# Norm sums as column-tiled matmuls with a high and a low part, and attention's norms moved from the score stage into the output stage ahead of it

## The chip, the cores and the metric

One Trainium2 chip, the same program on all 8 cores (two dies of four), each core with its own sequence of the prompt group and its own 16 samples. The metric is the device time of the slowest core in microseconds. Executions come in a fast and in a slow state (in the slow one the cores of one die, in some runs of both, show a lower granted clock: the lowest core of each slow run has a mean of 0.811 to 0.971); every comparison below uses fast runs only.

## The reference, cut to what matters

Two layers, three sub-blocks each, every sub-block behind an RMSNorm over 1024 channels:

```python
def rmsnorm(x, g):
    xf = x.astype(jnp.float32)
    y = xf * lax.rsqrt(jnp.mean(xf * xf, axis=-1, keepdims=True) + EPS)
    return (y * g.astype(jnp.float32)).astype(x.dtype)
# per layer:
#   x = x + mixer(rmsnorm(x))          layer 0 pooling, layer 1 gated short convolution
#   x = x + mem_attend(rmsnorm(x))     256 memory tokens, 4 heads
#   x = x + sq_relu_mlp(rmsnorm(x))
```

## The kernel before

x lies in SBUF with channels on partitions, as 8 chunks of 128 channels by 2064 tokens, and is worked off in 5 tiles of 416 tokens (the last 400, 16 of them samples). The sum of squares over channels is a sum over partitions, so TensorE makes it: a 128x128 matrix of ones times the squared chunks, eight matmuls accumulating in one PSUM bank. Every partition of the bank then holds the same sum, and ScalarE turns it into `exp(-0.5*ln(sum/D + eps))`.

```python
    def norm_a(ti, U, n=None, parts=1):            # squares, on ACT
        ...
            act(U(sl(a, a + w), sl(0, n)), X(sl(a, a + w), sl(c0, c0 + n)), AF.Square)

    def norm_b(ti, grow, U, RSTD, n=None):
        norm_r(ti, U, RSTD, n)
        norm_s(ti, grow, U, RSTD, n)

    def norm_r(ti, U, RSTD, n=None):               # sums on PE, then ln and exp on ACT
        n = n or TILES[ti][1]
        bk = nxt()
        for c in range(NCH):
            mm(PSv(bk, 0, n), ONESB(), U(c, sl(0, n)), c == 0, c == NCH - 1)
        act(PSv(bk, 0, n), PSv(bk, 0, n), AF.Ln, scale=1.0 / D, bias=EPS)
        act(RSTD(sl(0, n)), PSv(bk, 0, n), AF.Exp, scale=-0.5)

    def norm_s(ti, grow, U, RSTD, n=None, cs=range(NCH)):   # scaling, eight DVE instructions
        for c in cs:
            stt(U(c, sl(0, n)), X(c, sl(c0, c0 + n)), G(c, sl(grow, grow + 1)), RSTD(sl(0, n)), ALU.mult, ALU.mult)
```

There are 25 such norms on a core: 1 in the prelude (attention's norm of the first tile), 18 for attention and MLP of the two layers, 6 in the conv stage. `nxt()` hands out PSUM banks in rotation. Attention runs as score stages S(k) (eight blocks m) and output stages O(k-1) (eight column blocks ec), interleaved. Small pieces hang between blocks; one is `step`, which starts a sample's attention, with eight dot products on DVE:

```python
        for k in range(NT):
            def mid_s(m, k=k):                     # after block m of score stage S(k)
                ...
                if k == 0:
                    ...
                    if m == 1:
                        N2a(1)                     # squares
                    if m == 4:
                        N2b(1)                     # sums and scaling
                    return
                if m == 2:
                    N2b(k + 1) if k + 1 < NT else N3b(0)
                ...
                if m == 5:
                    step()
            S(k, mid_s)
            ...
            if k > 0:
                O(k - 1, lambda ec: (trickle() if ec % 2 == 0 else pre() if ec == 1 else step() if ec == 3 else None))
```

The sample attention already uses column tiling: four matmuls with 16 output columns each, into four groups of 32 PSUM partitions:

```python
        def SB(b):
            for x in range(2):
                for h in range(4):
                    mmx(V(PS[32 * h:32 * h + NS, OBK, 0:257], ...), PBZ[b % 2](x * 4 + h), VS[b % 2](x, h, sl(0, 257)), ...)
```

In the conv stage each channel block c is 24 matmuls; DVE has a chain of six to eight instructions per block, and its last product (`gate`) frees the block's last PSUM bank.

The softmax here doesn't subtract the row's maximum and nothing guards it: scores larger than these inputs give would overflow.

Of the kernel before, what the change touches and what calls it, by code (L numbers as in the profile page):

```python
# [8 lines left out]
BF16 = mybir.dt.bfloat16  # L9
# [122 lines left out]
def build_program():  # L132
# [99 lines left out]
    def sl(a, b):  # L232
        return slice(a, b)

    def PSv(bank, a, b, m=128):
        return V(PS[0:m, bank, a:b], [(PSB + bank * 2048, PSB + (bank + 1) * 2048)], excl=True)
# [11 lines left out]
    def nxt():  # L248
        b = bank_ctr[0] % bank_mod[0]
        bank_ctr[0] += 1  # L250
        return b
# [39 lines left out]
    def mm(out, lhsT, rhs, start, stop):  # L291
        P.add(PE, "c", lambda e, o=out.ap, l=lhsT.ap, r=rhs.ap: e.matmul(out=o, lhsT=l, rhs=r, start=start, stop=stop),  # L292
              [lhsT, rhs], [out])
# [19 lines left out]
    def act(out, in_, func, scale=1.0, bias=0.0):  # L313
        rd = [in_]
        sc = scale
        if isinstance(scale, V):
            rd.append(scale)
            sc = scale.ap
        P.add(ACT, "c", lambda e, o=out.ap, i=in_.ap: e.activation(out=o, in_=i, func=func, bias=bias, scale=sc), rd, [out])  # L319
# [87 lines left out]
    def trickle():  # L407
        if pieces:
            name, kc = pieces.pop(0)
            if kc == 0:  # L410
                claim(name)
            dma(POOL, W(name)(kc), DV(wsrc_sq(wsrc[name])[:, kc, :]), f"w{slot_of[name]}")
# [10 lines left out]
    def norm_a(ti, U, n=None, parts=1):  # L423
        c0 = TILES[ti][0]
        n = n or TILES[ti][1]
        w = NCH // parts
        for a in range(0, NCH, w):
            act(U(sl(a, a + w), sl(0, n)), X(sl(a, a + w), sl(c0, c0 + n)), AF.Square)

    def norm_b(ti, grow, U, RSTD, n=None):  # L430
        norm_r(ti, U, RSTD, n)
        norm_s(ti, grow, U, RSTD, n)

    def norm_r(ti, U, RSTD, n=None):
        n = n or TILES[ti][1]
        bk = nxt()
        for c in range(NCH):
            mm(PSv(bk, 0, n), ONESB(), U(c, sl(0, n)), c == 0, c == NCH - 1)
        act(PSv(bk, 0, n), PSv(bk, 0, n), AF.Ln, scale=1.0 / D, bias=EPS)
        act(RSTD(sl(0, n)), PSv(bk, 0, n), AF.Exp, scale=-0.5)  # L440

    def norm_s(ti, grow, U, RSTD, n=None, cs=range(NCH)):
# [19 lines left out]
    def prelude():  # L462
# [238 lines left out]
        for k in range(4):  # L701
            extra[13 + k].append(lambda k=k: kv("wk0", mk_d, k))
        extra[11].append(lambda: norm_a(0, BUF[0], parts=2))
        extra[12].append(lambda: norm_r(0, BUF[0], RSTDE))
        for i in range(4):
            extra[13 + i].append(lambda i=i: norm_s(0, R_ATTN, BUF[0], RSTDE, cs=(2 * i, 2 * i + 1)))
        stA(0)
# [104 lines left out]
    def conv_nA(ti):  # L812
        norm_a(ti, CUT[ti % 2], parts=2)

    def conv_nB(ti):
        norm_b(ti, R_MIX + 1, CUT[ti % 2], RSTDQ)

# [64 lines left out]
    def conv_phase():  # L882
        conv_begin()
        for ti in range(NT):
            def mid(c, ti=ti):
                if c == 0 and ti:
                    conv_out(ti - 1)
                if ti == 0 and c == 2:
                    conv_state()
                if ti == 1 and c == 1:  # L890
                    conv_state2()
                if c == 2:
                    if ti == NT - 1:
                        norm_a(SEQS[1][0], BUF[0], parts=2)
                    elif ti:
                        conv_nA(ti + 1)
                if c == (4 if ti else 1):
                    first_norm(1, RSTDQ) if ti == NT - 1 else conv_nB(ti + 1)

            conv_in(ti, mid)  # L900
        free("cin_b")
        load("wq1")
# [18 lines left out]
    def attn_phase(l, fill=()):  # L921
# [26 lines left out]

        def N2a(k):
            norm_a(seq[k], BT[k % 2])  # L950

        def N2b(k):
            norm_b(seq[k], R_ATTN + l, BT[k % 2], RSTD)
# [35 lines left out]
        def O(k, mid):  # L989
            c0, _, n, _ = TILES[seq[k]]  # L990
            pt = PT[k % 2]
            for ec in range(NCH):
                bk = nxt()
                for m in range(NCH):
                    mm(PSv(bk, 0, n), VWO(m, sl(ec * 128, (ec + 1) * 128)), pt(m, sl(0, n)), m == 0, m == NCH - 1)
                tt(X(ec, sl(c0, c0 + n)), PSv(bk, 0, n), X(ec, sl(c0, c0 + n)), ALU.add)
                mid(ec)
# [100 lines left out]
        def N3a(ti):  # L1098
            norm_a(ti, BT[1] if ti == 0 else U3[ti], TILES[ti][2])

        def N3b(ti):
            norm_b(ti, R_FFN + l, BT[1] if ti == 0 else U3[ti], RSTDM if ti > 1 else RSTD, TILES[ti][2])

# [20 lines left out]
        def stB(q, ti, j, mid=None, cols=None):  # L1124
            c0, n, npmt, ns = TILES[ti]
            n = npmt if q == 0 else n
            a0, a1 = cols or (0, n)
            Wd = W(f"dn{l}_{q}")
            h = H[j % 2]
            for ec in range(NCH):  # L1130
                bk = nxt()
                for fc in range(NCH):
                    mm(PSv(bk, 0, a1 - a0), Wd(fc, sl(ec * 128, (ec + 1) * 128)), h(fc, sl(a0, a1)), fc == 0, fc == NCH - 1)
                tt(X(ec, sl(c0 + a0, c0 + a1)), PSv(bk, 0, a1 - a0), X(ec, sl(c0 + a0, c0 + a1)), ALU.add)
                if mid is not None:
                    mid(ec)
# [11 lines left out]
        def step():  # L1148
            if todo:
                todo.pop(0)[1]()  # L1150

        def pre():
            if todo and todo[0][0] is not None:
                todo[0][0]()

        for k in range(NT):
            def mid_s(m, k=k):
                if m % 2 and k:
                    trickle()
                if l == 0 and (k == 1 or k == 0 and m > 3):  # L1160
                    late.pop(0)()
                if k == 0:
                    if l == 1 and m == 1:
                        conv_tail()
                    if m == 1:
                        N2a(1)
                    if m == 4:
                        N2b(1)
                    if l == 1 and m == 6:
                        conv_tail2()  # L1170
                    return
                if m == 2:
                    N2b(k + 1) if k + 1 < NT else N3b(0)
                if l == 0 and k == 1:
                    return
                if m == 3:
                    pre()
                if m == 5:
                    step()

            if k == 1:
                QSAMP()
                if l == 0:
                    free("wv0")
                    load_slowly("dn0_0")
            S(k, mid_s)
            if l == 0 and k == 1:
                free("wo0")
                load_slowly("up0_1")
                SDK(0)  # L1190
                SDV(0)
            if k + 2 < NT:
                N2a(k + 2)
            elif k + 2 == NT:
                N3a(0)
            if k > 0:
                O(k - 1, lambda ec: (trickle() if ec % 2 == 0 else pre() if ec == 1 else step() if ec == 3 else None))
        SDK(n_att)

        def mid_o(ec):  # L1200
            if ec == 0:
                N3a(1)
            if ec % 2 == 0:
                trickle()
            if ec == 1:
                pre()
            if ec == 3:
                step()
            if ec == 5:
                N3b(1)  # L1210

        O(NT - 1, mid_o)
# [38 lines left out]
        for j, (q, ti) in enumerate(items):  # L1251
            if q == 0 and ti + 2 < NT:
                N3a(ti + 2)
            if j + 1 < len(items):
                q1, t1 = items[j + 1]
                stA(q1, t1, j + 1, mid_m)
                if t1 == NT - 1 and q1:
                    free(f"up{l}_{q1}")
                    if q1 < 3:
                        load(f"dn{l}_{q1 + 1}")  # L1260
            if q == 0 and ti + 2 < NT:
                N3b(ti + 2)
            yield ("A", j)
            if l == 1 and j == len(items) - 1:
                stB(q, ti, j, mid_m, (TAIL, n_last))
                yield ("T", j)
                stB(q, ti, j, mid_m, (0, TAIL))
            else:
                stB(q, ti, j, mid_m)
            if ti == NT - 1 and q:  # L1270
                free(f"dn{l}_{q}")
                if q < 2:
                    load(f"up{l}_{q + 2}")
            yield (q, ti)
# [34 lines left out]
    for at in attn_phase(0, kv1_fill()):  # L1309
        if at == ("A", 16):  # L1310
            conv["cin_c"] = load_u("cin_c", 0)
        if at == ("A", 18):
            conv["cin_h"] = load_u("cin_h", 1)
            load("cout")
            conv_nA(1)
        if at == (3, 2):
            conv_nA(0)
        if at == ("A", 18):
            conv_nB(0)
    conv_phase()  # L1320
    done = [0]
# [146 lines left out]
```

## Time and profile before

| | before |
|---|---|
| time, median of fast runs | 1622.3 us (first four runs) |
| PE busy | 97% |
| norm: PE time held by the eight matmuls | 1.41 us at 416 columns (1.30 to 1.35 on narrower tiles), 25 times |
| PE waits of all kinds between 110 and 1500 us, slowest core | about 7 us |

PE bounds this kernel.

The timeline of before, PE only, around one group of column-tiled sample matmuls (start, duration, group, count).

```profile
299.71 4.56 PE L292 MATMUL PS<-MEM 128*128 128x416 bf16 x25
304.20 0.40 PE L296 MATMUL PS<-MEM 128*16 128x257 bf16 x8
304.53 13.37 PE L292 MATMUL PS<-MEM 16*128 16x512 bf16 x74
```

Eight matmuls of 257 columns hold PE for 0.33 us, from 304.20 to 304.53. One after another they would take about 8 x 0.11 us (an estimate from the 176 ns from start to start at 416 columns). In the records four start 3 to 4 ns apart and the next four 113 ns after these. So four really run side by side. The extra time on entering and leaving comes once per group: 270 ns from the start before to the first of them, where 176 is usual, and 206 ns from the last to the next start, where 257 columns would take about 110 by the same estimate.

### The profile page before, as it was taken

Reading aid. Unit: us, or ns where it says so; the run is one execution under the profiler, and the core shown is the slowest. Engines: PE = TensorE matmul, PEld = TensorE weight load, DVE = VectorE, ACT = ScalarE, POOL = GpSimd, SP = SyncE. Lnnn points to the kernel's source line nnn. Section 1 sums busy time; section 2 is a strip of 40 time slices with the busy share of each in tenths; the row PEclk is TensorE's granted clock in tenths of the full one; section 3 lists DMA queues with packets and bytes.
Section 4 is the critical chain, followed back from the end, with each engine's and each line's share of the span. In section 5 each row is a group of like instructions: output and inputs, shape, how many; then the busy total and the mean of one; then the engine's idle time right before and its main releaser. Section 6 shows DMA issues by size and latency. Waiting matters only on the chain.

```text
span 1620.1 us, 28511 instructions; the slowest of 8 cores (1616.6 to 1620.1 us)
## 1 busy us (share of the span) xinstructions
PE 1568.4 (97%) x10162; PEld 912.5 (56%) x10168; DVE 848.8 (52%) x1899; ACT 555.8 (34%) x1046; POOL 113.7 (7%) x245
## 2 busy tenths in 40 slices
PE   4899999999999999999999999999999999999997
PEld 3775555555556655555555555555555655555565
DVE  4666675655443444445666664767465444442325
ACT  4755435441121221222223224533643112213453
POOL 2002121110000000000000001121110000000000
PEclk9999999999999999999999999999999999999999
DMA  8979793665537706067000009694555663000112
GB/s 221 211 123 170 153 189 61 122 141 84 85 65 130 120 1 105 14 92 109 1 1 1 0 1 170 118 205 94 120 118 73 97 105 53 14 1 1 40 66 106
DMA packets 87189, 145.13 MB, mean 90 GB/s; under 512 B 4350, under 2 KB 41470, under 8 KB 87036
## 3 DMA queue, kind: packets, MB, share of 16 engines
q0 software_dynamic: 67568, 84.08, 36.0%
q1 hardware_dynamic: 19484, 59.24, 11.0%
q8 instruction: 84, 1.38, 0.3%
q14 instruction: 53, 0.43, 0.1%
HBM read 212.42 MB, written 14.36 MB: 140 GB/s over the span
## 4 chain that ended last, share of the span: by engine, by line
PE 91%; DVE 2%; ACT 2%; DMA 2%; issue 2%; POOL 0%; DVEq 0%; ACTq 0%; SPq 0%; POOLq 0%
PE PS L292 88%; PE PS L296 2%; DVE MEM L327 2%; ACT MEM L319 1%; DMA MEM<-gv 1%; PE PS L301 1%; DMA MEM<-x 1%; ACT MEM L308 1%; DVE MEM L331 0%; DVE MEM L345 0%; DVE MEM L339 0%; ACT MEM L343 0%; POOL MEM L354 0%; DVEq L1362 0%; ACTq L1362 0%
## 5 line engine op out<-in xcount | busy, mean ns | idle before, releaser
L292 PE MATMUL PS<-MEM 128*128 128x416 bf16 (+5 forms) x9082 | 1495.1, 325 | 11.6 <-ACT MEM L319 3.9
L292 PEld LDWEIGHTS PS<-MEM 128*128 128x128 bf16 x9088 | 844.0, 98 | 650.6 <-issue 42.1
L319 ACT ACTIVATE MEM<-PS 128x416 f32<-128x416 f32 (+5 forms) x469 | 238.6, 510 | 650.1 <-PE PS L292 639.4
L331 DVE TENSOR_TENSOR MEM<-PS,MEM 128x416 f32<-128x416 f32 (+6 forms) x533 | 297.7, 574 | 264.7 <-PE PS L292 256.4
L331 DVE TENSOR_TENSOR MEM<-MEM 128x416 bf16<-128x416 f32 (+3 forms) x282 | 159.8, 583 | 196.9 <-ACT MEM L319 188.4
L327 DVE SCALAR_TENSOR_TENSOR MEM<-MEM 128x416 bf16<-128x416 f32 (+7 forms) x322 | 176.9, 601 | 128.7 <-ACT MEM L319 109.0
L319 ACT ACTIVATE MEM<-MEM 128x416 bf16<-128x416 f32 (+9 forms) x299 | 184.9, 630 | 147.7 <-DVE MEM L331 112.6
L304 DVE SCALAR_TENSOR_TENSOR MEM<-MEM,PS 128x256 f32<-128x256 f32 x256 | 105.1, 420 | 72.6 <-PE PS L292 49.4
L343 ACT COPY MEM<-PS 128x512 f32<-128x512 f32 (+3 forms) x73 | 39.1, 535 | 134.8 <-PE PS L292 121.6
L296 PE MATMUL PS<-MEM 128*128 128x128 bf16 (+4 forms) x896 | 60.7, 248 | 16.7 <-DVE MEM L339 7.8
L296 PEld LDWEIGHTS PS<-MEM 128*128 128x128 bf16 (+2 forms) x896 | 49.0, 107 | 30.3 <-issue 29.5
L345 DVE CAST MEM<-PS 128x512 bf16<-128x512 f32 (+1 forms) x68 | 43.0, 654 | 12.1 <-PE PS L292 12.1
L354 POOL DMA_DIRECT2D MEM<-cv x64 | 47.6, 744 | 13.8 <-PE PS L292 13.5
L343 ACT CAST MEM<-PS 128x512 bf16<-128x512 f32 (+3 forms) x57 | 30.7, 548 | 48.7 <-PE PS L292 47.9
L319 ACT ACTIVATE PS<-PS 128x416 f32<-128x416 f32 (+3 forms) x67 | 33.1, 494 | 40.0 <-PE PS L292 39.6
L327 DVE SCALAR_TENSOR_TENSOR MEM<-PS,MEM 128x1024 f32<-128x1024 f32 (+1 forms) x17 | 21.8, 1283 | 44.3 <-ACT MEM L319 44.3
L301 PE MATMUL PS<-MEM 128*128 128x128 f32 (+5 forms) x184 | 24.7, 275 | 16.9 <-DMA MEM<-gv 7.1
L351 POOL MEMSET MEM<- 128x4 bf16 (+1 forms) x96 | 15.0, 159 | 357.8 <-PE PS L296 307.5
L301 PEld LDWEIGHTS PS<-MEM 128*128 128x128 f32 (+5 forms) x184 | 20.5, 143 | 20.0 <-issue 18.5
L354 POOL DMA_DIRECT2D MEM<-w_up x36 | 20.6, 582 | 131.9 <-PE PS L292 131.9
L339 DVE TENSOR_SCALAR MEM<-MEM 128x1024 bf16<-128x1024 f32 (+1 forms) x18 | 17.9, 997 | 22.7 <-ACT MEM L319 22.7
L354 POOL DMA_DIRECT2D MEM<-w_down x22 | 13.8, 635 | 207.2 <-PE PS L292 163.1
(28 smaller groups left out, 137.4 us busy)
## 6 DMA issues: line engine op xcount, KB each, us to landing
MEM<-ck SPq DMA_DIRECT2D x64, 512.0 KB, 6.2
MEM<-cv POOLq DMA_DIRECT2D x64, 256.0 KB, 6.1
MEM<-w_down POOLq DMA_DIRECT2D x6, 2048.0 KB, 17.9
MEM<-x SPq DMA_DIRECT2D x16, 512.0 KB, 12.5
MEM<-w_kv POOLq DMA_DIRECT2D x4, 2048.0 KB, 19.0
MEM<-w_o POOLq DMA_DIRECT2D x4, 2048.0 KB, 24.6
MEM<-w_up POOLq DMA_DIRECT2D x32, 256.0 KB, 13.2
MEM<-w_up POOLq DMA_DIRECT2D x4, 2048.0 KB, 17.9
```

Of the source, the lines that this page charges most:

```text
L292: P.add(PE, "c", lambda e, o=out.ap, l=lhsT.ap, r=rhs.ap: e.matmul(out=o, lhsT=l, rhs=r, start=start, stop=stop), [lhsT, rhs], [out])
L296: P.add(PE, "c", lambda e, o=out.ap, l=lhsT.ap, r=rhs.ap: e.matmul(out=o, lhsT=l, rhs=r, start=start, stop=stop, is_transpose=is_transpose ...
L301: P.add(PE, "c", lambda e, o=out.ap, i=in_.ap, d=ident.ap: e.transpose(out=o, in_=i, identity=d), [in_, ident], [out])
L304: P.add(DVE, "c", lambda e, o=out.ap, a=in0.ap, b=in1.ap, c=acc.ap: e.scalar_tensor_tensor(out=o, in0=a, scalar=1.0, in1=b, op0=ALU.mult, ...
L308: P.add(ACT, "c", lambda e, o=out.ap, i=in_.ap, a=acc.ap: e.activation(out=o, in_=i, func=AF.Square, accum_out=a), [in_], [out, acc])
L319: P.add(ACT, "c", lambda e, o=out.ap, i=in_.ap: e.activation(out=o, in_=i, func=func, bias=bias, scale=sc), rd, [out])
L327: P.add(eng, "c", lambda e, o=out.ap, a=in0.ap, b=in1.ap: e.scalar_tensor_tensor(out=o, in0=a, scalar=sc, in1=b, op0=op0, op1=op1), rd, [out])
L331: P.add(eng, "c", lambda e, o=out.ap, a=in0.ap, b=in1.ap: e.tensor_tensor(out=o, in0=a, in1=b, op=op), [in0, in1], [out])
L339: P.add(eng, "c", lambda e, o=out.ap, a=in0.ap: e.tensor_scalar(out=o, in0=a, scalar1=sc, scalar2=None, op0=op0), rd, [out])
L343: P.add(ACT, "c", lambda e, o=out.ap, i=in_.ap: e.copy(out=o, in_=i), [in_], [out])
L345: P.add(eng, "c", lambda e, o=out.ap, i=in_.ap: e.tensor_copy(out=o, in_=i), [in_], [out])
L354: return P.add(q, "d", lambda e, o=out.ap, i=in_.ap: e.dma_start(out=o, in_=i), [in_], [out], chan=chan, after=after)
```

## The change

The intent: summing over partitions needs only one useful output column, so eight matmuls of 128 columns make the same sum 128 times. Take 32 columns, run four chunks side by side in four column groups, in two passes. This leaves four partial sums on the four partition groups. Split them into a bf16 high part (ACT copy) and a bf16 low part (DVE subtraction), and add and broadcast them with two full ones-matmuls. The sums are split in time: `norm_p` first, `norm_r` with the scaling some blocks later. Attention's norms also move from score stage S(k+1) into output stage O(k-1).

```diff
+    def norm_p(ti, U, RSTD, n=None):
+        n = n or TILES[ti][1]
+        bk = nxt()
+        for i in range(2):
+            for h in range(4):
+                mmx(V(PS[32 * h:32 * h + 32, bk, 0:n], PSv(bk, 0, 1).ivs, True), ONESB(sl(0, 32)), U(4 * i + h, sl(0, n)), i == 0, i == 1)
+        hi, lo = [T(RSTD.off + i * n * 2, BF16, [n]) for i in range(2)]
+        cp(hi(), PSv(bk, 0, n), eng=ACT)
+        tt(lo(), PSv(bk, 0, n), hi(), ALU.subtract)
+
     def norm_r(ti, U, RSTD, n=None):
         n = n or TILES[ti][1]
         bk = nxt()
-        for c in range(NCH):
-            mm(PSv(bk, 0, n), ONESB(), U(c, sl(0, n)), c == 0, c == NCH - 1)
-        act(PSv(bk, 0, n), PSv(bk, 0, n), AF.Ln, scale=1.0 / D, bias=EPS)
+        for i in range(2):
+            mm(PSv(bk, 0, n), ONESB(), T(RSTD.off + i * n * 2, BF16, [n])(), i == 0, i == 1)
+        act(PSv(bk, 0, n), PSv(bk, 0, n), AF.Ln, scale=1.0 / (32 * D), bias=EPS)
...  prelude
-        extra[12].append(lambda: norm_r(0, BUF[0], RSTDE))
+        extra[12].append(lambda: norm_p(0, BUF[0], RSTDE))
+        extra[13].append(lambda: norm_r(0, BUF[0], RSTDE))
...  conv stage
-                if c == (4 if ti else 1):
+                if c == (3 if ti else 0):
+                    if ti == NT - 1:
+                        norm_p(SEQS[1][0], BUF[0], RSTDQ)
+                    else:
+                        conv_nP(ti + 1)
+                if c == (5 if ti else 2):
                     first_norm(1, RSTDQ) if ti == NT - 1 else conv_nB(ti + 1)
...  score stage
-                    if m == 4:
+                    if m == 3:
+                        N2p(1)
+                    if m == 5:
                         N2b(1)
...
-                if m == 2:
-                    N2b(k + 1) if k + 1 < NT else N3b(0)
+                if k == 1 and m == 0:
+                    N2p(2)
+                if k == 1 and m == 2:
+                    N2b(2)
...  output stage
-                O(k - 1, lambda ec: (trickle() if ec % 2 == 0 else pre() if ec == 1 else step() if ec == 3 else None))
+                def mid_k(ec, k=k):
+                    ...
+                    if ec == 3:
+                        step()
+                    if k < NT - 1:
+                        if ec == 4:
+                            N2p(k + 2) if k + 2 < NT else N3p(0)
+                        if ec == 6:
+                            N2b(k + 2) if k + 2 < NT else N3b(0)
+
+                O(k - 1, mid_k)
...  MLP part: N3p before an output stage, N3b after its second block (cut)
```

More of the change, by code (lines that the diff above doesn't have):

```diff
@@ L813, in conv_nA, with conv_nP @@
         norm_a(ti, CUT[ti % 2], parts=2)
+    def conv_nP(ti):
+        norm_p(ti, CUT[ti % 2], RSTDQ)
     def conv_nB(ti):
@@ L950, in N2a, with N2p @@
             norm_a(seq[k], BT[k % 2])
+        def N2p(k):
+            norm_p(seq[k], BT[k % 2], RSTD)
         def N2b(k):
@@ L1099, in N3a, with N3p @@
             norm_a(ti, BT[1] if ti == 0 else U3[ti], TILES[ti][2])
+        def N3p(ti):
+            norm_p(ti, BT[1] if ti == 0 else U3[ti], RSTDM if ti > 1 else RSTD, TILES[ti][2])
         def N3b(ti):
@@ L1196, in attn_phase @@
             if k > 0:
-                O(k - 1, lambda ec: (trickle() if ec % 2 == 0 else pre() if ec == 1 else step() if ec == 3 else None))
+                def mid_k(ec, k=k):
+                    if ec % 2 == 0:
+                        trickle()
+                    if ec == 1:
+                        pre()
+                    if ec == 3:
[6 more added lines that the diff above has]
+                O(k - 1, mid_k)
         SDK(n_att)
@@ L1208, in mid_o @@
                 step()
-            if ec == 5:
+            if ec == 4:
+                N3p(1)
+            if ec == 6:
                 N3b(1)
@@ L1260, in attn_phase @@
                         load(f"dn{l}_{q1 + 1}")
-            if q == 0 and ti + 2 < NT:
-                N3b(ti + 2)
+            nrm = q == 0 and ti + 2 < NT
+            if nrm:
+                N3p(ti + 2)
             yield ("A", j)
@@ L1268, in attn_phase @@
             else:
-                stB(q, ti, j, mid_m)
+                stB(q, ti, j, lambda c: (N3b(ti + 2) if nrm and c == 1 else None, mid_m(c)))
             if ti == NT - 1 and q:
@@ L1318, in build_program @@
         if at == ("A", 18):
+            conv_nP(0)
+        if at == (3, 3):
             conv_nB(0)
```

## The prediction

> **What bounds the kernel now.** TensorE. The page's busy table gives PE 97% (DVE 52%, ACT 34%), and the chain that ended last is 91% PE. In the timeline 128x416 matmuls start every 176 ns almost throughout; after the first 120 us, all start-to-start gaps over 130 ns beyond the nominal pitch add up to only about 11 us on core 4. So the time falls by roughly what leaves the PE stream, minus new waits.
>
> **What the change removes.** 25 norms per core each use eight full 128x416 ones-matmuls, which hold PE for 1.41 us (next instruction's start minus first start), nearly all without a wait: about 35 us.
>
> **What it puts there.** Eight 32-column matmuls in two passes of four, then two full matmuls (high and low part). The sample group's 128x257 matmuls are already column-tiled: four start 3 to 4 ns apart, the next four 113 ns later, so they really overlap. Going in costs 93 ns extra (269 ns from the previous 416-wide start, not 176), coming out 97 ns (206, not about 110). [...] My estimate for one norm: 93 + 180 + 180 + 97 for the sums and 352 for the two full ones, 0.90 us instead of 1.41. Saved: 0.5 us x 25 = 12.5 us.
>
> **What it adds elsewhere.** Per norm one ACT copy (about 0.52 us) and one DVE subtraction (about 0.58 us). They cost only where PE catches up with the low part.
>
> **Where I expect some of it to be lost** (durations from the trace):
> - Output stages ahead (three per layer): at the fourth column block a sample's eight dot products (4.0 us on DVE) are queued before that stage's fifth eviction and the low part. The low part lands 0.25 to 0.6 us after PE wants it: about 2 us in all.
> - Last conv tile: DVE is already serial there (about 3.9 us per channel block against PE's 4.06), and the output projection waits for its last gate (waits of 1.16 and 1.29 us). The norm cannot save there, and the later place pushes that gate out: about 1 us lost.
> - Layer 1, first score stage: squares end 0.8 us before the sums are needed; the sums come one block (1.4 us) earlier: 0.7 us wait. The scaling, one block later, then ends after the sample query projection wants it: up to 0.9 us.
> - MLP part and middle conv tiles: the low part is ready 0.6 us or more ahead; no loss.
>
> Moving norms from score to output stage evens out DVE, but PE waits for no norm there today: no gain.
>
> **Sum.** 12.5 - 2 - 1 - 1.6 = 8 us, less an allowance: 1615 us (-0.5%), range 1610 to 1621. Faster by over 2%: 1%; within 2%: 98%; slower: 1%.
>
> **What would show it.** PE records: four starts within 12 ns, passes about 180 ns apart, drains of 90 to 100 ns at each side. New PE waits released by DVE at the low-part matmul in output stages, and by ACT squares at layer 1's first score stage.
>
> **What would make it wrong.** The four 416-wide streams not overlapping (then +9 us instead); a larger drain; long low-part waits (over 1 us each), making it flat, or none of my waits appearing (1610).

For one norm 93 + 180 + 180 + 97 + 352 ns = 0.90 us, and 12.5 - 2 - 1 - 1.6 = 8 us in all, with the allowance 1615 us. The 93, 97 and 352 ns (2 x 176) come from the trace of before; 180 per pass is an estimate from its 176 ns and the 3 to 4 ns between starts. "Drains" are the 93 and 97 ns.

## More of the kernel before

The prelude mixes the pooling mixer of layer 0 with the folding of weights (`wq_turn`, `foldk`): short matmuls that wait for PSUM evictions (1.75 us for a DVE copy at the first weight fold, core 5 of before).

From the page of before, slowest core: the busy line of part 1; the PE and granted-clock rows of part 2 (40 slices, tenths); the engine line of part 4, the chain that ended last.

```profile
PE 1568.4 (97%) x10162; PEld 912.5 (56%) x10168; DVE 848.8 (52%) x1899; ACT 555.8 (34%) x1046; POOL 113.7 (7%) x245
...
PE   4899999999999999999999999999999999999997
...
PEclk9999999999999999999999999999999999999999
...
PE 91%; DVE 2%; ACT 2%; DMA 2%; issue 2%; POOL 0%; DVEq 0%; ACTq 0%; SPq 0%; POOLq 0%
```

The waits view of before, PE only, 110 to 1500 us. Columns: who waited, for whom, us in total, how often, longest.

```profile
engine line waited for: us in total, times, longest us
PE PS L292 <- DVE MEM L331: 2.1, 2, 1.1
PE PS L296 <- ACT MEM L319: 2.0, 2, 1.1
PE PS L292 <- ACT MEM L319: 1.9, 8, 0.2
...
```

L292 is the helper of all ordinary matmuls, L331 the two-operand DVE instruction, L319 the ACT function. With the two smaller groups left out they come to 7.2 us, and none is at a norm.

Granted clock by core in before, from the view of the cores:

```profile
core: us from the first to the last instruction, mean granted TensorE clock
...
core 3: 1616.6 us, clock 0.995
core 4: 1620.1 us, clock 0.995
...
core 6: 1617.0 us, clock 0.994
...
```

All eight cores have 0.994 or 0.995, and the spans lie within 3.5 us.

## The result

| | before | after |
|---|---|---|
| median | 1622.3 us (4 runs) | 1620.15 us (4 runs, 1619.59 to 1620.44) |
| ratio of fast runs | | 0.9986, 95% interval 0.9969 to 1.0003 |

A ratio is the mean time of one kernel's fast runs over that of the other's of the same rounds, so it is not quite the ratio of the medians. The time fell by about 2.2 us, where 7.3 was predicted. The interval just includes no change, but all four runs of after lie below every fast run of before in this document (1621.1 to 1624.3).

The page of after, the lines that answer to those above:

```profile
PE 1562.5 (97%) x10218; PEld 901.6 (56%) x10218; DVE 864.4 (53%) x1924; ACT 567.3 (35%) x1071; POOL 113.8 (7%) x245
...
PE   4899999999999999999999998999999999999997
...
PEclk9899999999999999999999999999999999999999
...
PE 89%; DVE 4%; ACT 2%; issue 2%; DMA 2%; POOL 0%; DVEq 0%; ACTq 0%; SPq 0%; POOLq 0%
```

Three things differ: DVE has 2% more of the chain, the second slice of the clock row (40 to 81 us) is 8 instead of 9, and so is one slice of the PE row (from 970 us, around the last conv tile). The waits view of after (PE, 110 to 1500 us, slowest core):

```profile
PE PS L292 <- DVE MEM L331: 5.3, 9, 2.2
PE PS L296 <- ACT MEM L319: 3.0, 4, 1.1
PE PS L292 <- ACT MEM L319: 1.9, 8, 0.2
...
```

The waits for L331 went from 2 (2.1 us) to 9 (5.3 us), those of L296 for ACT from 2 to 4 (the two new ones are the sums waiting for the squares). The cores of after:

```profile
...
core 1: 1610.3 us, clock 0.995
core 2: 1610.9 us, clock 0.996
...
core 4: 1616.1 us, clock 0.991
core 5: 1618.0 us, clock 0.991
core 6: 1615.1 us, clock 0.991
...
```

Now the spans lie within 7.7 us. The fastest core is 6.3 us faster than any core in the profile of before, but three have a clock of 0.991 (the three left out: 0.995), and the time is that of the slowest core. From the first attention score stage to the first block of final rows:

| stretch (median of 8 cores, us) | before | after | predicted change | measured |
|---|---|---|---|---|
| layer 0 attention | 152.84 | 151.54 | -2.0 | -1.30 |
| layer 0 MLP up to conv | 494.50 | 492.51 | -2.0 | -1.99 |
| conv, up to the fourth output projection | 179.15 | 178.85 | -2.0 | -0.30 |
| last conv tile and first score stage of layer 1 | 69.85 | 70.73 | +0.7 | +0.88 |
| rest of layer 1 attention | 125.56 | 124.73 | -0.6 | -0.83 |
| layer 1 MLP | 389.04 | 387.76 | -1.5 | -1.28 |
| sum | 1410.9 | 1406.1 | -7.4 | -4.8 |

The predicted column is worked out from the terms of the prediction: 0.5 us per norm, and its four waits. In this sum all eight cores agree within about 0.1 us, in both kernels. So the spread is all in the prelude: the first score stage starts at 103.3 to 106.8 us before and at 101.7 to 109.5 us after. The worst core lost there 2.7 us of the 4.8 that every core gained later.

The windows view shows what happened on core 5, the slowest of after. The columns are the stretch, its length, busy us of PE, PEld, DVE, ACT, POOL (instructions), the granted clock, and DMA share with GB/s. First core 5 of before: the stretches are consecutive clock windows of 3.4 us, around the wait for rows of x and at the first weight fold.

```profile
63.60:67.00 3.40, 0.86 (x4) 0.32 (x4) 1.95 (x3) 3.24 (x4) 0.00 (x0) 0.99 1.05 236
67.00:70.40 3.40, 3.08 (x23) 2.32 (x24) 0.46 (x1) 3.12 (x9) 0.00 (x0) 0.50 1.04 245
70.40:73.80 3.40, 3.40 (x44) 3.20 (x43) 2.18 (x4) 2.42 (x6) 0.00 (x0) 1.00 0.95 186
87.45:90.86 3.41, 2.19 (x31) 1.72 (x29) 3.35 (x6) 2.54 (x5) 0.00 (x0) 1.00 0.24 79
90.86:94.28 3.42, 2.74 (x34) 2.42 (x35) 3.14 (x5) 2.10 (x6) 0.90 (x1) 1.00 0.48 60
94.28:97.69 3.41, 2.48 (x30) 2.08 (x28) 3.31 (x7) 2.03 (x5) 0.00 (x0) 1.00 1.11 205
```

Then core 5 of after:

```profile
63.68:67.09 3.41, 1.33 (x20) 1.02 (x17) 1.76 (x3) 3.23 (x6) 0.00 (x0) 1.00 1.08 247
67.09:70.50 3.41, 2.29 (x27) 1.86 (x24) 0.19 (x1) 3.29 (x6) 0.00 (x0) 0.50 1.03 216
70.50:73.92 3.42, 3.42 (x26) 3.15 (x25) 2.73 (x5) 2.43 (x6) 0.00 (x0) 0.50 1.05 271
91.00:94.40 3.40, 1.14 (x11) 0.64 (x8) 3.34 (x5) 2.67 (x7) 0.70 (x1) 1.00 0.09 21
94.40:97.80 3.40, 3.40 (x25) 2.77 (x24) 2.65 (x5) 0.82 (x2) 0.20 (x1) 0.50 0.33 38
97.80:101.20 3.40, 3.40 (x24) 2.78 (x23) 2.39 (x5) 1.52 (x3) 0.00 (x0) 0.50 1.09 149
```

Before, the window with 0.86 us of PE work is followed by one at clock 0.50, and so are those with 1.33 and 1.14 us after. Before, PE filled the half-clock window (3.08 of 3.40 us, the last four of the norm's eight matmuls among it) and the clock came back. After, the window at 67.09 was filled for only 2.29 us and the clock stayed at half. At the fold the emptiest window had 1.14 us of PE work, and two half-clock windows followed, the first of them busy throughout.

What I call a clock window is read from the clock records in the packed traces of before and after: every stretch of one clock in them is a whole multiple of 3.413 us long (from 1 to 458 times), except the last, which begins at 1603 us or later and runs past the program's end. The half-clock stretches between 45 and 1600 us last 3.41 or 6.83 us, at a granted clock of 0.50. Where the grid lies differs from core to core: in before one of them begins at 66.95 us on core 5 and at 68.44 on core 2. Of the half-clock windows that begin between 45 and 100 us in these two profiles, 17 were followed by full clock, with PE busy for 81% to 100%. Six were followed by another at half clock, all on cores 4 to 6 of after: three with 66% to 67% and three with 100%. Why those at 100% did not end it, no run shows. On how busy PE was in the windows ahead of them, see e6.

### The profile page after: what moved, and what is told of

The parts are those of the page before. It is cut to its first block, busy times and chain, and to the rows that moved or that the text cites. A ratio compares the mean times of both kernels' runs of the same rounds, so it can differ in the third digit from the quotient of the medians.

```text
span 1618.0 us, 28570 instructions; the slowest of 8 cores (1610.3 to 1618.0 us)
## 1 busy us (share of the span) xinstructions
PE 1562.5 (97%) x10218; PEld 901.6 (56%) x10218; DVE 864.4 (53%) x1924; ACT 567.3 (35%) x1071; POOL 113.8 (7%) x245
## 4 chain that ended last, share of the span: by engine, by line
PE 89%; DVE 4%; ACT 2%; issue 2%; DMA 2%; POOL 0%; DVEq 0%; ACTq 0%; SPq 0%; POOLq 0%
PE PS L292 85%; PE PS L296 3%; DVE MEM L327 3%; ACT MEM L319 2%; PE PS L301 1%; DMA MEM<-gv 1%; DMA MEM<-x 1%; DVE MEM L331 1%; ACT MEM L308 1%; DVE MEM L304 0%; DVE MEM L345 0%; POOL MEM L354 0%; DVEq L1409 0%; ACT MEM L343 0%; ACTq L1409 0%
## 5 line engine op out<-in xcount | busy, mean ns | idle before, releaser
L292 PE MATMUL PS<-MEM 128*128 128x416 bf16 (+7 forms) x8938 | 1477.5, 325 | 12.4 <-DVE MEM L331 5.3
L292 PEld LDWEIGHTS PS<-MEM 128*128 128x128 bf16 (+1 forms) x8938 | 828.7, 98 | 647.9 <-issue 54.8
L331 DVE TENSOR_TENSOR MEM<-PS,MEM 128x416 f32<-128x416 f32 (+6 forms) x558 | 312.2, 575 | 296.0 <-PE PS L292 260.7
L331 DVE TENSOR_TENSOR MEM<-MEM 128x416 bf16<-128x416 f32 (+3 forms) x282 | 160.4, 584 | 224.6 <-ACT MEM L319 205.3
L327 DVE SCALAR_TENSOR_TENSOR MEM<-MEM 128x416 bf16<-128x416 f32 (+7 forms) x322 | 177.0, 601 | 60.1 <-ACT MEM L319 50.2
L296 PE MATMUL PS<-MEM 128*128 128x128 bf16 (+6 forms) x1096 | 75.2, 267 | 18.1 <-DVE MEM L339 7.3
L296 PEld LDWEIGHTS PS<-MEM 128*128 128x128 bf16 (+3 forms) x1096 | 52.9, 105 | 40.4 <-issue 39.3
L343 ACT CAST MEM<-PS 128x512 bf16<-128x512 f32 (+6 forms) x82 | 43.2, 531 | 90.5 <-PE PS L292 50.7
L319 ACT ACTIVATE PS<-PS 128x416 f32<-128x416 f32 (+2 forms) x67 | 33.2, 496 | 50.8 <-PE PS L292 50.8
L345 DVE CAST MEM<-PS 128x512 bf16<-128x512 f32 (+1 forms) x68 | 43.3, 656 | 12.5 <-PE PS L292 12.3
L327 DVE SCALAR_TENSOR_TENSOR MEM<-PS,MEM 128x1024 f32<-128x1024 f32 (+1 forms) x17 | 21.8, 1283 | 44.5 <-ACT MEM L319 44.5
L301 PE MATMUL PS<-MEM 128*128 128x128 f32 (+5 forms) x184 | 25.0, 277 | 18.3 <-DMA MEM<-gv 8.4
```

The source lines that it names most:

```text
L292: P.add(PE, "c", lambda e, o=out.ap, l=lhsT.ap, r=rhs.ap: e.matmul(out=o, lhsT=l, rhs=r, start=start, stop=stop), [lhsT, rhs], [out])
L296: P.add(PE, "c", lambda e, o=out.ap, l=lhsT.ap, r=rhs.ap: e.matmul(out=o, lhsT=l, rhs=r, start=start, stop=stop, is_transpose=is_transpose ...
L301: P.add(PE, "c", lambda e, o=out.ap, i=in_.ap, d=ident.ap: e.transpose(out=o, in_=i, identity=d), [in_, ident], [out])
L319: P.add(ACT, "c", lambda e, o=out.ap, i=in_.ap: e.activation(out=o, in_=i, func=func, bias=bias, scale=sc), rd, [out])
L327: P.add(eng, "c", lambda e, o=out.ap, a=in0.ap, b=in1.ap: e.scalar_tensor_tensor(out=o, in0=a, scalar=sc, in1=b, op0=op0, op1=op1), rd, [out])
L331: P.add(eng, "c", lambda e, o=out.ap, a=in0.ap, b=in1.ap: e.tensor_tensor(out=o, in0=a, in1=b, op=op), [in0, in1], [out])
```

## The experiments

"First score stage to end" in the expectations is the time from the first score stage's first matmul to the last matmul: 1506.6 us before, 1501.6 after. It contains the stretch of the table and the kernel's tail. The tail proved to vary by up to 1.3 us between kernels for reasons of its own (its last blocks wait for the vector part of the final rows: on the chain of before, core 4, from 1600 to 1617 us, that is 1.1 us for two instructions of ACT and 1.3 us for one of DVE at a time), so I give the table's stretch too (1410.9 before, 1406.1 after). "Low-clock cores" counts core executions in fast runs with a mean clock of 0.9925 or less: 4 of 136 in before (16 fast runs of the two later sessions and the profiled run), 17 of 32 in after (3, 6, 4 and 4 in its four runs). The sessions are comparable: the fast runs of before have a median of 1622.5 us in the one of e1 to e4 and 1622.1 in that of e5 to e8.

### e1_prelude_old: one norm of 25 put back

```diff
-        extra[12].append(lambda: norm_p(0, BUF[0], RSTDE))
-        extra[13].append(lambda: norm_r(0, BUF[0], RSTDE))
+        extra[12].append(lambda: norm_o(0, BUF[0], RSTDE))   # the eight full matmuls, scale 1/D
```

> The changed kernel with one of its 25 norms, the one in the prelude, put back to eight full matmuls. On the traces, everything after the first score stage takes 1506.6 us before and 1501.6 us after on all eight cores, but the prelude got longer on some cores, which ran in half-clock windows of 6.8 us at about 65 and 92 us (before: 3.4 us). Theory A: the prelude's new sums let the clock fall for longer, so with the old sums there no core shows the 6.8 us window at 65 us, mean clock is 0.994 or more on all cores, and the time is about 1617 us (before minus 5). Rival B: the windows fall by chance whatever the kernel: still about half the cores at 0.991, time 1619 to 1620.

Measured: 1616.9, 1617.3, 1616.9 and 1617.0 us in the fast runs, ratio 0.9967 (0.9954 to 0.9981). Low-clock cores: 2 of 32. The details of the expectation were too strict: two cores of the profiled run had 0.992, one had a 6.8 us half-clock window at 61 us, and four still had one of 3.4 or 6.8 us after 85 us. But the time is the expected one, and it is 3.1 us below after, with one norm of 25 changed. The stretch is 1405.7 us.

### e2_prelude_only: that one norm alone

```diff
-        extra[12].append(lambda: norm_r(0, BUF[0], RSTDE))
+        extra[12].append(lambda: norm_p2(0, BUF[0], RSTDE))  # the new sums, into the kernel before
+        extra[13].append(lambda: norm_r2(0, BUF[0], RSTDE))
```

> The kernel before with the new sums in the prelude's one norm only. The time from the first score stage to the end should be 1506.6 us as before. Theory A: some cores get the 6.8 us half-clock windows (clock about 0.991) and the time is 1624 to 1625 us, slower than before. Rival B: clocks and time as before, 1622.

Measured: median of the five fast runs 1624.1 us (1621.6 to 1625.5), ratio 1.0007 (0.9994 to 1.0021), so slower by about a microsecond but not clear of noise in the time alone. The clocks are clear: 12 of 40 low-clock cores against 4 of 136, and in the profile seven of eight cores have a 6.8 us half-clock window starting between 90 and 95 us, where no core of before has one (three cores of e1 do, with the old sums, so the mean clocks over many runs count for more than one profile). The stretch is 1410.8 us, as before. Rival B is out by the clocks; of theory A the clocks are shown, the loss of time only in the changed kernel (e1).

### e3_conv_split: the conv norm's scaling in two bursts

```diff
-                if c == (5 if ti else 2):
-                    first_norm(1, RSTDQ) if ti == NT - 1 else conv_nB(ti + 1)
+                if c in ((5, 6) if ti else (2, 3)):          # norm_r and chunks 0-3, then chunks 4-7
+                    ...
```

> The changed kernel with the conv stage's norm scaling (eight DVE instructions, 4.6 us in one burst) split into two bursts of four, one channel block apart. Theory: the new waits of 0.36 to 0.49 us near the end of each conv tile come from that burst holding up the gate product that frees a PSUM bank; split, they go away and the four middle conv tiles take about 0.4 us less each, so first score stage to end is about 1500 us. Rival: the waits come from the extra PSUM bank in the rotation or from the sums' new places; then they stay and that stretch stays at 1501.6.

Measured: the stretch is 1406.2 us, no gain; the time is 1618.0, 1619.4, 1621.5 and once 1634.3 us (with two cores of one die at a clock of 0.977), with 6 of 32 low-clock cores. The waits view shows why (PE, 110 to 1500 us):

```profile
PE PS L292 <- DVE MEM L327: 2.6, 8, 1.1
PE PS L292 <- DVE MEM L331: 2.0, 4, 1.0
```

L331 includes the gate product, L327 is the scaling. In after PE waited for L331 nine times and for L327 once (0.2 us); now it waits for the scaling itself, in pairs of about 0.2 and 0.39 us at the start of the next tile. The wait for a bank did go away, so the burst did cause it, but the second half of the scaled input now comes too late. As posed, neither theory is right: the norm has no slack at that block, however the scaling is cut.

### e4_attn_in_score: attention's norms back in the score stage

```diff
-                if k == 1 and m == 0:
-                    N2p(2)
-                if k == 1 and m == 2:
-                    N2b(2)
+                if m == 0:
+                    N2p(k + 1) if k + 1 < NT else N3p(0)
+                if m == 2:
+                    N2b(k + 1) if k + 1 < NT else N3b(0)
...
-                    if k < NT - 1:
-                        if ec == 4:
-                            N2p(k + 2) if k + 2 < NT else N3p(0)
-                        if ec == 6:
-                            N2b(k + 2) if k + 2 < NT else N3b(0)
```

> The changed kernel with the attention's norms put back into the score stage (sums at its first block, the two full matmuls at its third), everything else as changed. Theory: in the output stage the low part waits behind a sample's dot products on DVE (PE waits of 0.24 to 0.58 us, six in all, 2.2 us); moved back these waits go away, and first score stage to end is about 1499.5 us instead of 1501.6. Rival: the move pays by taking ACT and DVE work out of the score stage; then the score stages get new waits and the stretch is 1501.6 or more.

Measured: the stretch is 1404.3 us. The two attention parts are 1.16 and 1.01 us shorter than in after, and no new wait appears in the score stages, so the move cost 2.2 us; 0.35 us of that is lost again in the conv stage, by a cause I did not follow. The time is 1618.6 us (median of three fast runs), still with 10 of 24 low-clock cores. The waits view:

```profile
PE PS L292 <- DVE MEM L331: 4.3, 5, 1.9
PE PS L296 <- ACT MEM L319: 3.3, 4, 1.0
```

From nine waits for L331 to five. How such a wait comes about is seen in after, core 5, in its first output stage (timeline, DVE and then PE):

```profile
164.75 0.42 DVE L304 SCALAR_TENSOR_TENSOR MEM<-MEM,PS 128x256 f32<-128x256 f32 x1
165.10 0.08 DVE L304 DVE_READ_ACCUMULATOR MEM<-MEM,PS 128x1 f32 x1
165.10 2.08 DVE L331 TENSOR_TENSOR MEM<-PS,MEM 128x416 f32<-128x416 f32 x4
```

```profile
162.51 0.54 PE L296 MATMUL PS<-MEM 128*32 128x416 bf16 x8
162.97 3.16 PE L292 MATMUL PS<-MEM 128*128 128x416 bf16 x17
166.33 1.92 PE L292 MATMUL PS<-MEM 128*128 128x416 bf16 x10 [0.19 <-DVE MEM L331]
```

The dot products hold DVE until about 165.1, then comes an eviction, then the low part, the second instruction of the group of four. The second of the two full matmuls cannot start before 166.33. By start-to-start times this wait is 0.35 us.

### e5_conv_early: the conv norm one block earlier, and split

```diff
-                if c == (5 if ti else 2):
-                    first_norm(1, RSTDQ) if ti == NT - 1 else conv_nB(ti + 1)
+                if c in ((4, 5) if ti else (1, 2)):          # norm_r and chunks 0-3, then chunks 4-7
+                    ...
```

> The changed kernel with the conv stage's two full matmuls and scaling one channel block earlier (the block at which the kernel before had its norm) and the scaling split into two bursts of four. Splitting alone gained nothing: the wait for a PSUM bank turned into a wait for the second half of the scaled input. Theory: at the later block the norm has no slack left; earlier and split, both waits go away, the middle conv tiles give back about 0.4 us each, and first score stage to end is about 1500.0 us instead of 1501.6. Rival: the conv stage is paced by DVE as a whole, so PE time saved there is lost wherever the norm is put; then 1501.6 stays.

Measured: the stretch is 1404.6 us, 1.5 less than after; the conv part alone is 177.44 us instead of 178.85. First score stage to end is 1501.1, because the tail was 1.0 us longer in this kernel. The time is 1619.9 us with 14 of 32 low-clock cores. The theory holds for the stage: the four middle tiles give back 1.4 us. Rival out. The last conv tile did not gain.

### e6_filler: useless matmuls in the empty window

```diff
                         c = 4 * hp + 2 * hh + j
+                        if dc == 0 and c == 4:
+                            for i in range(NCH):
+                                mm(PSv(bk, 0, TW), ONESB(), W("wq0")(i, sl(0, TW)), True, True)
                         mm(PSv(bk, hh * 256, (hh + 1) * 256), wt(c), TR(c), j == 0, j == 1)
```

> The changed kernel with eight useless full matmuls (about 1.4 us of PE work, results overwritten) put into the PE wait of about 2 us in the prelude's first weight fold. [...] the emptiest such window at the fold is 44% busy before and in the run with the old prelude sums, 34% after. Theory: what costs the time is how empty that window is, so filling it lifts it well over 46%, no core shows a half-clock window after 85 us, few cores have a mean clock of 0.9925 or less (17 of 32 in the changed kernel's runs, 4 of 80 before), and the time falls to 1617 to 1618 us with more work on PE. Rival: the extra ACT and DVE work of the prelude's norm delays the cores by itself, or the half clock comes from the wait for the rows of x at 53 to 67 us; then clocks and time stay at 1619 to 1620.

(The 46% is from the count below, and its windows are the steps of the clock records. The 44% and 34% are the emptiest 3.4 us at any position at the fold.)

Measured: median of five fast runs 1618.2 us (1617.8 to 1620.3), ratio 0.9978 (0.9965 to 0.9991); 4 of 40 low-clock cores instead of 17 of 32. No core has a half-clock window between 85 us and the end of the prelude; three have a 3.4 us one at 972 to 976 us, at the last conv tile's wait. So PE does more work and the kernel takes 2 us less. PE timeline of core 5 at the fold: before, after, and with the filler.

```profile
89.19 0.60 PE L292 MATMUL PS<-MEM 128*128 128x256 bf16 x4 [0.15 <-ACT MEM L343]
91.54 0.60 PE L292 MATMUL PS<-MEM 128*128 128x256 bf16 x4 [1.75 <-DVE MEM L345]
```

```profile
91.41 0.60 PE L292 MATMUL PS<-MEM 128*128 128x256 bf16 x4 [0.26 <-DVE MEM L327]
94.00 0.69 PE L292 MATMUL PS<-MEM 128*128 128x256 bf16 x4 [2.00 <-DVE MEM L345]
```

```profile
92.34 2.00 PE L292 MATMUL PS<-MEM 128*128 128x256 bf16 x12 [0.15 <-ACT MEM L343]
95.08 0.60 PE L292 MATMUL PS<-MEM 128*128 128x256 bf16 x4 [0.73 <-DVE MEM L345]
```

The change lengthened the two waits from 0.15 and 1.75 us to 0.26 and 2.00. That is only 0.36 us, but it moves the emptiest possible 3.4 us window here from 44% to 34% busy (worked out from the records, sliding the window; the same on every core of a kernel), and more positions of the windows hit it: shifted over all positions, 58% give a window below 46% here, against 30% before. With the filler the emptiest is 73%. The 46% comes from a count in the prelude: over all ten profiles, 80 cores, 45 to about 100 us, I compared the PE-busy share of every full-clock window with what came after:

```
busy share of a 3.4 us window    followed by half clock
under 46%                        90 of 90
46% to 55%                       13 of 73
over 55%                         0 of about 1000
```

In before and after alone it is 15 of 15, 2 of 11 and 0 of 197. This is a count for the prelude and no rule. Near the last conv tile (966 to 976 us) 14 windows of 40% to 46% were followed by full clock (one of them in after, core 4 at 972.9 us, 40%), and only three of 38%, all in this run, by half. What else decides there, no run shows.

The filler reaches 1618.2 and e1 1617.0. So filling the window takes the half clock away from the fold. It does not tell how much of this norm's loss lies there, as e8 shows below. What remains is in line with the other place, the half-clock windows near 66 us, of which the filler's profile has two of 6.8 us: the new sums no longer fill them (PE was busy for 66% to 67% of the first 3.4 us in after, on the three cores that had 6.8 us; for 81% to 100% in before). I did not test that place by itself.

### e7_mended and e8_mended_filler: all three mended

e7 is the three edits e1, e4 and e5 together; e8 adds the filler of e6.

> Together: old sums in the prelude's norm, attention's norms in the score stage, conv's norm one block earlier and split; the new column-tiled sums in the other 24. If the three causes add up: first score stage to end about 1498.0 us (1501.6 less 2.0 and 1.6), time about 1613.5 us, against 1622.5 before.

> The mended kernel with the eight filler matmuls as well. Theory of the empty window: half-clock windows after 85 us (3 of 8 cores even with the old prelude sums) go away, the spread between cores narrows, time about 1612.5 us. Rival: filler changes nothing, 1613.5.

Measured: e7 1614.6 us (median of four fast runs, 1614.0 to 1615.2), ratio 0.9953 (0.9939 to 0.9967), low-clock cores 2 of 32, stretch 1402.4 us. The causes add up: from after's 1406.1, the gains of e1, e4 and e5 (0.4, 1.8 and 1.5) give 1402.4. The time is 1.1 us above what was expected, since the tail was 0.6 us longer and five of eight cores of the profile still had a half-clock window after 90 us. e8: 1613.1 us (median of five, 1612.0 to 1614.1), ratio 0.9942 (0.9928 to 0.9956), low-clock cores 0 of 40, stretch 1402.1. The filler again takes off 1.5 us, here with the old sums in the prelude, and no core has a half-clock window after 85 us. e8 beats both given kernels, by 9 us over before.

## Why the prediction was right or wrong

**What bounds the kernel, and the cost of one norm: right.** Estimated 0.90 us instead of 1.41. In after the four starts lie within 10 ns, the second pass comes 186 ns after the first, going in costs 93 ns and coming out 96 (272 ns from the last start, not 176), so with the two full matmuls 0.91 us.

**Waits for the low part in the output stages: right.** Predicted 0.25 to 0.6 us each, about 2 us in all. Measured six waits of 0.24 to 0.58 us; undoing the move gave 2.2 us back (e4). "No gain" from moving was right as well.

**Last conv tile, layer 1's first score stage: right in size.** Predicted +0.7 us for that stretch, measured +0.88. The wait for squares was 0.79 us (predicted 0.7), that of the sample query projection 0.5 (up to 0.9).

**MLP: right.** No loss, as predicted.

**The step that failed first: "Saved: 0.5 us x 25 = 12.5 us", for the one norm in the prelude.** I counted it like the 24 others. In the changed kernel it cost about 3 us instead (1620.15 against 1617.0 in e1); put alone into the kernel before it cost about 1 us, not clear of noise (e2). Its new sums leave PE less busy in a part that waits for rows of x, for evictions and for DVE (2.29 against 3.08 us in the half-clock window near 67 us on core 5; 34% against 44% in the emptiest 3.4 us at the fold). In that part all 90 windows under 46% busy were followed by half clock, and none of about 1000 over 55% (table of e6). The view of the cores showed 0.994 to 0.995 and not 1.0 before, so half-clock windows existed; I did not ask where they lay and what kept them short. As the time is that of the slowest of eight cores, and the windows lie differently from core to core (66.95 us on core 5, 68.44 on core 2 of before), a loss on half of the cores is the whole loss. What is shown: this one norm causes it (e1, e2). Over all fast runs, 59 of 160 core executions with the new sums in the prelude and no filler have a low clock (after, e2, e3, e4, e5), against 8 of 200 with the old sums (before, e1, e7).

How the loss divides between the two places is only argued. From the records of the cores that have them all: at the fold a half-clock window of 6.8 us costs about 2.1 us (fold to first score stage 17.8 to 18.3 us, without one 15.8 to 16.2). Near 66 us it costs about 1 us more than one of 3.4 (norm to the first `wq_turn` 23.1 to 23.6 us, otherwise at most 22.4). The fold is hit with the old sums too (6.8 us on four of eight cores in e7's profile), and the filler gains 1.5 us there (e8) against 1.9 with the new sums (e6). So the 1.9 us is not this norm's share. Of the fourteen windows of 6.8 us near the first place twelve are in profiles with the new sums (the two others begin at 60.6 and 63.0 us, before the norm), and the ten of these twelve cores that have no filler were all hit at the fold as well. The first place therefore carries a part that no run here isolates; the old sums together with the filler, in after, would have told. What stays open too: why the fold's wait grew by 0.36 us. In the traces I looked at, one DVE copy of the last key projection starts 0.42 us after its wait was passed, before 0.06 us after, with nothing on record between.

**The second: "MLP part and middle conv tiles: ... no loss", for the conv tiles.** Predicted -2.0 us, measured -0.30. I checked only that the low part comes in time, not what the scaling behind it does: eight instructions, 4.6 us on DVE, after which the next block's gate product runs, whose bank PE wants soon after. In after, core 4 (DVE, then PE), the scaling, the gate product and the matmul that waits for its bank:

```profile
826.88 4.58 DVE L327 SCALAR_TENSOR_TENSOR MEM<-MEM 128x416 bf16<-128x416 f32 x8
834.39 0.59 DVE L331 TENSOR_TENSOR MEM<-PS,MEM 128x416 bf16<-128x416 f32 x1
835.13 2.09 PE L292 MATMUL PS<-MEM 128*128 128x416 bf16 x11 [0.19 <-DVE MEM L331]
```

Before, that product ended about 0.2 us ahead of PE's need (833.38 against 833.59 us on core 4). Counted from the first of the norm's full matmuls, PE now comes there 1.06 us sooner, as they hold it for 0.35 instead of 1.41 us, but the product ends only 0.64 us sooner (10.41 us after it against 11.05). So PE waits, by start-to-start times 0.36 to 0.49 us per tile. The order of blocks around the scaling is the same in both kernels, one block apart: by this reckoning it is the shorter hold that makes this wait, not the later place (no run tests the two apart). The later place is what makes the scaled input late once the burst is split. Split alone the wait only changed its object (e3); earlier and split it went (e5, 1.4 us back).

**A smaller one:** layer 0's first score stage lost 0.5 us to the same wait for squares that I had named for layer 1 only. I took its slack as 2.8 us and the sums as one block earlier, but a piece of key projection hangs between the two places as well.

Together: 3 + 1.7 + 0.5 is about the 5 us that were missing.

## What to carry to other kernels

Cutting work from TensorE in a stretch where it already waits can slow it down: here one norm of 25 made 3.1 us of difference (e1). Look there at how busy PE is in each window of the clock records (3.4 us in this case), on all cores, before and after, and let a sparse stretch alone, or fill it; count in your own traces what is followed by half clock. A norm's matmuls can also be the time in which other engines catch up (in the middle conv tiles they went 1.06 us shorter, and the product behind them ended only 0.64 us sooner). When such a block shrinks or moves, follow the DVE burst behind it to the next PSUM bank and to the next consumer, not only its own inputs. On eight cores the slowest counts, so a random loss on some cores is the full loss.
